# Gating two feed-forward blocks at once, with another order and other sums for the seven-product form

## The chip, the core and the metric

The kernel runs on one core of one Trainium2 chip. The core has a matrix engine (TensorE, PE in the profile, with its weight loads as PEld), a vector engine (VectorE, DVE), an activation engine (ScalarE, ACT), a general engine (GpSimd, POOL), a queue engine that issues transfers (SyncE, SP), and 16 DMA engines. Work is held in SBUF; matrix products go to PSUM, eight banks of 512 float32 columns in each of 128 partitions. The metric is the device time of one execution in microseconds (us), and less is better.

## What is computed

Two layers, each made of a feed-forward half, a mixer and a second feed-forward half, on 256 positions of 1024 channels in float32:

```python
D_MODEL, SEQ, DEPTH, D_FF = 1024, 256, 2, 2816

def rms_norm(x, g):
    return x * lax.rsqrt(jnp.mean(x * x, axis=-1, keepdims=True) + EPS) * g

def swiglu(h, w_gate_up, w_down):
    a, b = jnp.split(h @ w_gate_up, 2, axis=-1)
    return (jax.nn.silu(a) * b) @ w_down

def hybrid_layer(x, ...):
    x = x + 0.5 * swiglu(rms_norm(x, ffn1_norm), ffn1_w_gate_up, ffn1_w_down)
    h = rms_norm(x, mix_norm)
    z = h @ w_in                       # u, q, k, v and two gates
    y_pool = multiscale_pool(u, pool_w, pool_scale)
    y_attn = moba_attention(rope(rms_norm(q)), rope(rms_norm(k)), v)
    merged = gate0 * (y_pool @ w_branch_pool) + gate1 * (y_attn @ w_branch_attn)
    x = x + merged @ w_out
    return x + 0.5 * swiglu(rms_norm(x, ffn2_norm), ffn2_w_gate_up, ffn2_w_down)
```

The change lies in the feed-forward halves. There are four of them, called stages 1 to 4 here; mixers stand between stages 1 and 2 and between 3 and 4, so stage 3 follows stage 2 directly.

## The kernel before

**Precision.** Every float32 operand of a product is split into a high part (`hi`, the operand in a reduced float32 format) and the rest (`lo`). ACT writes the high part as a copy, DVE writes the rest as a subtraction (`split`, L173 and L174; `halves`, L245 and L246, for activations). A product is then a matmul of the high weights with high and low activations side by side (512 columns) and one of the low weights with the high activations (256 columns), in `chain`.

**The feed-forward half.** The 2816 inner channels are 22 blocks of 128. A block has one weight unit of 1 MB (gate and up columns). `unit` hands out the next split unit, `fetch` issues the next load on SP into one of four `raw` buffers and splits it in two halves; the split parts have room for three units, so a unit can be split once the unit three places earlier has been multiplied. `pair` multiplies a block (32 matmuls) into two PSUM banks, and `drain` brings it to SBUF: ACT copies the part from the low activations (L222), DVE adds the rest (L223), into a tile `ab` of gate (256 columns) and up (256 columns). `post` gates a block: DVE scales both halves by the norm factor `r` (L398), ACT takes Silu of the gate half (L400), DVE multiplies it with the up half (L401), and `halves` splits the product into one of the tiles `ga` (blocks 0 to 7), `gc` (8 to 11), `gd` (12 to 15) and `gb` (16 to 21). The factor `r` comes from the sum of squares `acc` by two matmuls against ones (`factor_spread`, also per token in `factor_tokens`). The down projection then runs over 8 output rows f, and for each over all 22 blocks; `add_x` (L566 on) adds half of each row to `x`, and `prep` (L284, L285, L293, L294) makes the next stage's input `hx` from it. That input is not yet scaled by the norm factor, which is why `r` comes after the product.

**The forms.** In stages 2 to 4 blocks 12 to 15 are not multiplied directly. They are a 2 by 2 product of blocks (two token halves, two halves of the 1024 input channels, two column pairs), done with seven products instead of eight, Strassen's method in Winograd's form. The seven are called "1" to "7" and cost 16 matmuls each. The weight sums that they need are made by the DMA: `sum_form` sends a quadrant of the weights from POOL's queue into a buffer, later quadrants with addition (`accum_op`), and after each sum has been split the next one is added on top. Buffer "a" lies where `gd` will be and serves forms 1, 5, 6 and 4 in this order; buffer "b" lies in `gb` and serves 3 and 7; form 2 is a plain load. The sums of x (`x_forms`, L443 on) are made after block 3: eight ACT copies (L447), four DVE sums (L451 to L454) and four splits (L458, L459). `strassen` multiplies a form (`by_tokens`) into a PSUM bank and combines the products on DVE in SBUF tiles `p1`, `p5` and `c35`; `gated` gates a quarter of the result (L485, L486), and `turned` transposes two quarters back on PE into `gd` (L493 to L496). `feed_order` holds the order of blocks and forms.

**The order of the work.** PE's order is the program's. The other engines' order is worked out ahead by a planner, which takes what it holds to be ready, by the place in the program; `behind` forbids it to place one operation ahead of another. On the chip each engine's queue then runs in that order, and an operation that waits holds all that stands behind it.

**Buffers.** `ab` tiles come from five buffers of 512 columns (tag "t512"), which the mixer's temporaries use as well; in stage 1 eight more lie in the tile of the mixer's gates. `uT`, the mixer's pooling input, has a place of its own.

Of the kernel before, what the change touches and what calls it, by code (L numbers as in the profile page):

```python
# [25 lines left out]
P = 128  # L26
# [20 lines left out]
GROUP = 12  # L47
XF = 3
SHIFT = 16
FIRST = 5  # L50
FORMS = {
    "1": ("a", False, "11"), "3": ("b", False, "22"), "2": ("c", False, "21"), "5": ("a", True, "12"),
    "7": ("b", True, "12"), "6": ("a", True, "22"), "4": ("a", True, "21"),
# [3 lines left out]
def feed_order():  # L57

    return [0, 1, 2, 3, 4, 5, "1", 6, "3", 7, "2", 8, "5", 9, "7", 10, 11, "6", 16, 17, 18, "4", 19, 20, 21]
# [10 lines left out]
def trunk_kernel(ctx: ExitStack, tc: tile.TileContext, x_in, w_in, pw_in, qkn_in, rope_in, mask_in, band_in, out):  # L70
# [35 lines left out]

    plan = []
    for base in (0, FU, LU, LU + FU):
# [30 lines left out]
    sums_at = {}  # L139

    def sum_form(base, f):

        n = base + GROUP
        q = {"11": (n, 0), "12": (n + 2, 0), "21": (n, 1), "22": (n + 2, 1)}
        at, add, src = FORMS[f]
        if at == "c":
            sums_at["c"] = raws.tile([P, 2 * HALF], F32, name="raw", tag="raw")
        z = sums_at[at].rearrange("p (i c) -> p i c", i=2)
        u, kh = q[src]
        w = w_in[u:u + 2, :, kh * HALF:(kh + 1) * HALF].rearrange("u p c -> p u c")  # L150
        if add:
            nc.gpsimd.dma_start(z, w, accum_op=OP.add)
        elif at == "c":
            nc.sync.dma_start(z, w)
        else:
            nc.gpsimd.dma_start(z, w)
        _, hi, lo = buffers(False)
        z = z.rearrange("p i (k c) -> p i k c", c=2 * P)
        for h in range(2):
            a = z[:, :, 2 * h:2 * h + 2, :]  # L160
            hv, lv = (t[h].rearrange("p (k i c) -> p i k c", i=2, c=2 * P) for t in (hi, lo))
            act(hv, a, AF.Copy)
            tt(lv, a, hv.bitcast(F32), op=OP.subtract)
        return hi, lo
# [102 lines left out]
    uT = const.tile([P, NW, PAD + S], F32, name="uT")  # L267
    nc.gpsimd.memset(uT[:, :, :PAD], 0.0)
# [95 lines left out]

    def bc2(a):
        return a.unsqueeze(1).to_broadcast([P, 2, a.shape[-1]])

    def ffn(after, n0=0, end=False, col=None):
# [6 lines left out]

        room("ga", 0, 8)
        room("gc", 8, 4)
        abs_, more = {}, []

        def wide(n):  # L380
            if n0 and len(abs_) in range(5, 13):
                if not more:
                    more.extend(eight(F32, "ab"))
                abs_[n] = more.pop(0).rearrange("p (a s) -> p a s", s=S)
            else:
                abs_[n] = tmp.tile([P, 2, S], F32, name="ab", tag="t512", bufs=5)
            return abs_[n]
# [8 lines left out]
        def post(n):  # L396
            ab = abs_[n]
            scaled = tt(ab, ab, bc2(r[0]), op=OP.mult)  # L398
            sg = small.tile([P, S], F32, name="sg", tag="sg", bufs=2)
            act(sg, ab[:, 0, :], AF.Silu)  # L400
            tt(sg, sg, ab[:, 1, :], op=OP.mult)  # L401
            halves(gs[n], sg)
            return scaled

        if n0:
            room("gd", 12, 4)
# [6 lines left out]
            for i in range(n0 + 1, NF + 1):  # L413
                if i < NF:
                    pair(unit(), wide(i))
                    fetch()
                todo = range(done, min(done + (2 if i % 3 == 2 else 1), i) if i < NF else NF)
                done = todo.stop
                for n in todo:
                    scaled = post(n)  # L420
                    if i == n0 + 1:
                        behind(scaled, drained[-1])
        else:
# [9 lines left out]
            sums_at["a"] = acts.tile([P, 2 * HALF], F32, name="sa", tag="gd")  # L433
            pre = acts.tile([P, 12 * S], F32, name="pre", tag="gb")
            sums_at["b"] = pre[:, :NK * S]
            vt = acts.tile([P, 2, GW], F32, name="vt", tag="v")
            tk = [acts.tile([P, 2, GW], F32, name="tk", tag="tok", bufs=2) for _ in range(2)]
            p1, p5, c35 = tk[0][:, 0], tk[0][:, 1], tk[1][:, 0]
            xg = [t.rearrange("p a (b s) -> p (a b) s", s=S) for t in tk]
            gq = {tn: vt[:, tn // 2, tn % 2 * S:(tn % 2 + 1) * S] for tn in range(4)}  # L440
            sf = {}

            def x_forms():  # L443

                late = drained[-1]
                for k in range(NK):
                    behind(act(xg[k // 4][:, k % 4, :], x[:, k, :], AF.Copy, scale=gain[:, l_of[0], col + k:col + k + 1]), late)  # L447
                (a11, a21), (a12, a22) = ([z[:, :, t * P:(t + 1) * P] for t in range(2)] for z in xg)
                s1, s2 = (pre[:, (8 + 2 * i) * S:(10 + 2 * i) * S].rearrange("p (k s) -> p k s", s=P) for i in range(2))
                s3, s4 = (vt[:, i, :].rearrange("p (k s) -> p k s", s=P) for i in range(2))  # L450
                tt(s1, a22, a21, op=OP.subtract)  # L451
                stt(s2, s1, -1.0, a11, op0=OP.mult, op1=OP.subtract)
                tt(s3, a11, a21, op=OP.subtract)
                stt(s4, s2, -1.0, a12, op0=OP.mult, op1=OP.subtract)  # L454
                fs = iter(eight(F32R, "sf", SHIFT))
                for n, z in (("5", s1), ("3", s4), ("6", s2), ("7", s3)):
                    sh, sl = (next(fs).rearrange("p (k s) -> p k s", s=P) for _ in range(2))
                    act(sh, z, AF.Copy)  # L458
                    tt(sl, z, sh.bitcast(F32), op=OP.subtract)  # L459
                    sf[n] = [(sh[:, k, :], sl[:, k, :]) for k in range(4)]  # L460
                for n, k0, t in (("1", 0, 0), ("2", 4, 0), ("4", 4, 1)):
                    sf[n] = [tuple(hx[:, k, j, t * P:(t + 1) * P] for j in range(2)) for k in range(k0, k0 + 4)]
# [17 lines left out]
            def gated(c, t, n, sign):  # L480
# [5 lines left out]
                stt(by_half(gq[2 * t + n]), c[:, :, 1, :], sc, by_half(sg), op0=OP.mult, op1=OP.mult)  # L486

            def turned(n):
# [5 lines left out]
                g = gt["gd"][:, 2 * n:2 + 2 * n]  # L494
# [5 lines left out]
            def strassen(f):  # L500

                b = {"1": "a", "2": "a", "5": "e", "3": "h", "6": "g", "7": "f", "4": "f"}[f]
                fresh = b not in bank
                if fresh:
                    bank[b] = quarter("p" + b).rearrange("p a s -> p (a s)")
                z = bank[b]
                by_tokens(f, z, fresh)
                if f == "1":
                    act(p1, z, AF.Copy)
                elif f == "2":  # L510
                    gated(z, 0, 0, 0)
                elif f == "5":
                    act(p5, z, AF.Copy)
                    tt(c35, bank["h"], p5, op=OP.add)
                elif f == "6":
                    tt(p1, z, p1, op=OP.add)
                    tt(c35, c35, p1, op=OP.add)
                    gated(c35, 0, 1, 1)
                    tt(p5, p5, p1, op=OP.add)
                    gated(p5, 1, 1, 1)  # L520
                elif f == "7":
                    tt(p5, z, p5, op=OP.add)
                    room("gb", 16, NF - 16)
                elif f == "4":
                    tt(p1, z, p1, op=OP.add)
                    gated(p1, 1, 0, 0)
                    room("gd", 12, 4)

            late = []
            wait = [0, 1]  # L530
            for i, n in enumerate(feed_order()[2:]):
                if isinstance(n, str):
                    strassen(n)
                    if n == "4":
                        late += [[1, 1], [2, 0]]
                    continue
                pair(unit(), wide(n))
                fetch()
                if n == XF:
                    x_forms()  # L540
                for m in wait[:2]:
                    post(m)
                wait = wait[2:] + [n]
                for z in late:
                    z[0] -= 1
                    if z[0] == 0:
                        turned(z[1])
            for m in wait:
                post(m)
        gs = [gs[n] for n in range(NF)]  # L550
        for b in range(NK * NF):
# [9 lines left out]
            if k == NF - 1:  # L561
                add_x(f, ps, f < NK - 1 or not end)
                after(f)

    def add_x(f, ps, two):
# [29 lines left out]
    def norm_rope(z, g):  # L595

        ms = small.tile([P, 2 * NH], F32, name="ms", tag="ms", bufs=2)
        for t in range(2):
            sq = tmp.tile([P, NH, DH], F32, name="sq", tag="t512", bufs=5)
# [9 lines left out]
        for t in range(2):  # L609
            zt = z[:, t, :].rearrange("p (h d) -> p h d", d=DH)  # L610
            tt(zt, zt, ri[:, t * NH:(t + 1) * NH].unsqueeze(2).to_broadcast([P, NH, DH]), op=OP.mult)
            sw = tmp.tile([P, NH, DH], F32, name="sw", tag="t512", bufs=5)
# [68 lines left out]
    def mix(l, after):  # L681
# [12 lines left out]
        nc.sync.dma_start(pw, pw_in[l])  # L694
        gates = [z.rearrange("p (a s) -> p a s", s=S) for z in eight(F32, "gates")]
# [151 lines left out]
        def mixed(f):  # L847
            mg = tmp.tile([P, 2, S], F32, name="mg", tag="t512", bufs=5)
# [78 lines left out]
    for l in range(L):  # L927
        l_of[0] = l
        ffn(lambda f: prep(f, l, C_GM), len(w3) if l == 0 else 0, col=C_G1)
# [4 lines left out]
        if l + 1 < L:  # L934
            ffn(lambda f: prep(f, l + 1, C_G1), col=C_G2)
        else:
            ffn(lambda f: nc.sync.dma_start(out[:, f, :], x[:, f, :]), end=True, col=C_G2)
# [90 lines left out]
```

## Time and profile before

| | us |
|---|---|
| three runs | 1000.77, 1002.33, 2642.07 |
| their median | 1002.33 |
| the profiled execution | 1001.17 |
| its span | 999.4 |
| PE busy in it | 994.3 |
| DVE busy | 811.2 |
| ACT busy | 646.3 |

The span runs from the first to the last instruction of the profiled execution; the time of that execution is 1.77 us longer. Busy times of PE are modelled at their ends, so the chain of work that ended last says more than the busy share: it follows the last instruction back, at each step to what released it or to the instruction before it on its engine. In the timelines a row is the start, the duration, the engine, the line, what it writes and reads, and in brackets how long its engine had been idle before and who ended that. The rows of groups give count, total busy time and the mean of one in ns. The granted clock of PE is 1.00 in every stretch looked at.

Which stretch of time is which stage can be read from the chain: PE's product for the norm factor (two matmuls named `ss`) stands at 31.2, 334.8, 510.0 and 828.7 us, near the start of stages 1 to 4.

### The profile page before, as it was taken

The numbers are of one execution on the slowest core, as the hardware profiler recorded it, in microseconds if no ns is written. First come the engines' busy times: TensorE is split into PE (matmuls) and PEld (weight loads), VectorE is DVE, ScalarE is ACT, GpSimd is POOL, SyncE is SP. The second block draws the span as 40 slices with busy tenths as digits, with TensorE's granted clock in tenths as the row PEclk, the third lists the DMA queues.
The fourth block names the chain that finished last, engine by engine and source line by source line (L and its number), as shares of the span: only waits on it lengthen the run. The fifth ranks groups of instructions, "written<-read, shape, count | busy, mean of one in ns | idle before, by whom it ended". The sixth has DMA issues, their size and how long they took to land.

```text
span 999.4 us, 16145 instructions
## 1 busy us (share of the span) xinstructions
PE 994.3 (99%) x6336; PEld 903.0 (90%) x6336; DVE 811.2 (81%) x1220; ACT 646.3 (65%) x1026; POOL 35.1 (4%) x64
## 2 busy tenths in 40 slices
PE   9999999999999999999999999999999999999998
PEld 8888888898899988899998889998988999888988
DVE  6998866598978899886689988666988888989752
ACT  7876655567756786665578666556677567767541
POOL 0000000002000000000000000000020000000000
PEclk9999999999999999999999999999999999999999
DMA  8865555643556578765577876555544575785640
GB/s 296 313 211 204 204 188 207 206 150 140 194 204 250 184 173 282 211 210 184 197 259 175 283 205 212 182 202 184 188 179 178 171 255 177 225 223 202 223 148 22
DMA packets 34156, 202.34 MB, mean 202 GB/s; under 512 B 3488, under 2 KB 4768, under 8 KB 13088
## 3 DMA queue, kind: packets, MB, share of 16 engines
q1 hardware_dynamic: 29184, 182.44, 51.3%
q0 software_dynamic: 4896, 18.88, 9.0%
q8 instruction: 49, 0.80, 0.3%
q14 instruction: 27, 0.22, 0.1%
HBM read 200.26 MB, written 1.05 MB: 201 GB/s over the span
## 4 chain that ended last, share of the span: by engine, by line
PE 99%; DMA 0%; ACT 0%; DVE 0%; SPq 0%; issue 0%
PE ps L100 78%; PE pt L100 7%; PE two L100 4%; PE pe L100 2%; PE pa L100 2%; PE pf L100 2%; PE sc L100 1%; PE pg L100 1%; PE ph L100 1%; PE pt L667 1%; PE y L100 1%; DMA raw<-w 0%; PE tp L623 0%; PE pt L493 0%; PE st L100 0%; PE ss L100 0%
## 5 line engine op out<-in xcount | busy, mean ns | idle before, releaser
L100 PE MATMUL ps<-hx,hi 128*128 128x512 f32 x1504 | 507.0, 384 | 0.8 <-ACT hi L173 0.8
L174 DVE TENSOR_TENSOR lo<-raw,hi 128x1024 fp32r<-128x1024 f32 (+2 forms) x343 | 409.0, 1199 | 118.6 <-ACT hi L173 116.5
L173 ACT ACTIVATE hi<-raw 128x1024 fp32r<-128x1024 f32 (+2 forms) x343 | 352.1, 1035 | 201.5 <-PE ps L100 141.5
L100 PE MATMUL ps<-hx,lo 128*128 128x256 f32 x1504 | 411.1, 273 | 0.0
L100 PEld LDWEIGHTS ps<-hx,hi 128*128 128x128 f32 x1504 | 282.3, 188 | 51.3 <-ACT hi L173 1.1
L100 PEld LDWEIGHTS ps<-hx,lo 128*128 128x128 f32 x1504 | 282.6, 188 | 0.3 <-DVE lo L174 0.3
L100 PE MATMUL ps<-ga,hi 128*128 128x512 f32 (+1 forms) x264 | 87.0, 376 | 0.0
L100 PE MATMUL ps<-ga,lo 128*128 128x256 f32 x256 | 69.9, 273 | 0.0
L100 PE MATMUL ps<-gb,hi 128*128 128x512 f32 (+1 forms) x198 | 65.6, 376 | 0.0
L100 PE MATMUL pt<-hi,hx 128*128 128x512 f32 x192 | 65.1, 385 | 0.0
L100 PEld LDWEIGHTS ps<-ga,hi 128*128 128x128 f32 x264 | 49.0, 188 | 8.3
L398 DVE TENSOR_TENSOR ab<-ab,r 128x512 f32<-128x512 f32 x76 | 52.0, 687 | 0.9
L100 PE MATMUL pt<-lo,hx 128*128 128x256 f32 x192 | 52.6, 274 | 0.0
L100 PE MATMUL ps<-gb,lo 128*128 128x256 f32 x192 | 52.4, 273 | 0.0
L223 DVE TENSOR_TENSOR ab<-ps,ab 128x512 f32<-128x512 f32 x74 | 50.7, 686 | 0.9
L400 ACT ACTIVATE sg<-ab 128x256 f32<-128x256 f32 x76 | 31.3, 415 | 27.5 <-DVE ab L398 24.2
L100 PEld LDWEIGHTS ps<-ga,lo 128*128 128x128 f32 x256 | 48.1, 188 | 0.0
L100 PE MATMUL ps<-gc,hi 128*128 128x512 f32 (+1 forms) x132 | 44.3, 376 | 0.0
L100 PE MATMUL ps<-gd,hi 128*128 128x512 f32 (+1 forms) x132 | 44.3, 376 | 0.0
L100 PE MATMUL ps<-mk,hi 128*128 128x256 f32 x256 | 44.1, 275 | 0.0
L222 ACT ACTIVATE ab<-ps 128x512 f32<-128x512 f32 x74 | 43.0, 581 | 0.5 <-PE ps L100 0.5
L100 PEld LDWEIGHTS ps<-gb,hi 128*128 128x128 f32 x198 | 36.7, 188 | 6.2
(226 smaller groups left out, 1444.4 us busy)
## 6 DMA issues: line engine op xcount, KB each, us to landing
raw<-w SPq DMA_DIRECT2D x167, 1024.0 KB, 4.9
sa<-w POOLq DMA_DIRECT2D x12, 1024.0 KB, 9.8
pre<-w POOLq DMA_DIRECT2D x6, 1024.0 KB, 10.7
raw<-w SPq DMA_DIRECT2D x16, 256.0 KB, 5.3
out_dram<-gx SPq DMA_DIRECT2D x8, 128.0 KB, 1.9
gx<-x SPq DMA_DIRECT2D x3, 256.0 KB, 5.9
qk<-pw SPq DMA_DIRECT2D x2, 256.0 KB, 2.7
gx<-x SPq DMA_DIRECT2D x1, 300.0 KB, 2.8
```

Of the source, the lines that this page charges most:

```text
L100: return keep(nc.tensor.matmul(*args, **kw))
L173: act(hi, w, AF.Copy)
L174: return tt(lo, w, hi.bitcast(F32), op=OP.subtract)
L222: act(t, ps[:, :, 1, :], AF.Copy)
L223: drained.append(tt(t, ps[:, :, 0, :], t, op=OP.add))
L398: scaled = tt(ab, ab, bc2(r[0]), op=OP.mult)
L400: act(sg, ab[:, 0, :], AF.Silu)
L667: keep(nc.tensor.transpose(pt[:, h, o * P:(o + 1) * P], pr[:, h, c * P:(c + 1) * P], ident))
```

## The change

- `post` gates two blocks at once. Their `ab` tiles are one tile of 1024 columns, from two buffers (tag "t1k") and a third that shares its place with `uT`; in stage 1 four such tiles lie in the gates' tile. The splits of the product are written for two blocks by one ACT and one DVE operation. Blocks are gated in pairs, so the even block of a pair waits for the odd one.
- In stages 1 to 3 (`late_r`) only the gate half is scaled by `r`. The up half stays unscaled through the down projection, and `add_x` multiplies each output row by `r`, with one DVE operation more. The gated quarters of the forms leave out the same factor. In stage 4 both halves are scaled as before, for two blocks at once.
- The forms come in the order 1, 2, 7, 6, 5, 3, 4, the first after block 2 and the last ahead of block 11. Forms 1, 6, 5 and 3 are summed in one PSUM bank and read out in between; 2, then 7 and 4, in another.
- The weight sums lie in two buffers, "a" in the place of `gc` (form 1, then 5) and "b" in the place of `gd` (forms 7, 6 and 4). Form 7's sum takes two transfers; forms 2 and 3 are plain loads on SP.
- The sums of x are still made after block 3, but form 7's first; the copies lie in `pre` and not in `tk`. The transposes of the forms' results come in the middle of block 11 and after it, and were after blocks 19 and 20.
- The mixer's temporaries are halves of "t1k" tiles, and `uT` is allocated and its padding cleared in each mixer.

```diff
-    return [0, 1, 2, 3, 4, 5, "1", 6, "3", 7, "2", 8, "5", 9, "7", 10, 11, "6", 16, 17, 18, "4", 19, 20, 21]
+    return [0, 1, 2, "1A", 3, "2A", 4, "7A", 5, 6, 7, "6A", 8, "5A", 9, "3A", 10, "4A", 11, 16, 17, 18, 19, 20, 21]
...
+NEAR = {
+    "1": (("11",), "a"), "5": (("12",), "a"), "7": (("12", "22"), "b"), "6": (("11",), "b"), "4": (("21",), "b"),
+    "2": (("21",), ""), "3": (("22",), ""),
+}
...
+    def near_sum(base, f):
+
+        qs, at = NEAR[f]
+        z = two_rows(near[at])
+        for i, q in enumerate(qs):
+            kw = {} if i == 0 and f in "17" else {"accum_op": OP.add}
+            nc.gpsimd.dma_start(z, quadrant(base, "A", q), **kw)
+
+    def sum_form(base, n):
+
+        f, g = n
+        if g == "A" and NEAR[f][1]:
+            z = near[NEAR[f][1]]
+            _, hi, lo = buffers(False)
         else:
-            nc.gpsimd.dma_start(z, w)
+            z, hi, lo = buffers()
+            nc.sync.dma_start(two_rows(z), quadrant(base, g, NEAR[f][0][0]))
...
             act(hv, a, AF.Copy)
             tt(lv, a, hv.bitcast(F32), op=OP.subtract)
+        if g == "A":
+            if f in "176":
+                near_sum(base, {"1": "5", "7": "6", "6": "4"}[f])
...
+    def wide_tile(k):
+
+        if k % 3 < 2:
+            z = tmp.tile([P, 4 * S], F32, name="ab", tag="t1k", bufs=2)
+        else:
+            z = acts.tile([P, 4 * S], F32, name="ab", tag="uT")
+        return z.rearrange("p (b a s) -> p b a s", b=2, s=S)
...
         def post(n):
-            ab = abs_[n]
-            scaled = tt(ab, ab, bc2(r[0]), op=OP.mult)
-            sg = small.tile([P, S], F32, name="sg", tag="sg", bufs=2)
-            act(sg, ab[:, 0, :], AF.Silu)
-            tt(sg, sg, ab[:, 1, :], op=OP.mult)
-            halves(gs[n], sg)
+
+            ab = abs_[n // 2]
+            g, u = ab[:, :, 0, :], ab[:, :, 1, :]
+            if late_r:
+                scaled = tt(g, g, bc2(r[0]), op=OP.mult)
+            else:
+                z = ab.rearrange("p b a s -> p (b a) s")
+                scaled = tt(z, z, r[0].unsqueeze(1).to_broadcast([P, 4, S]), op=OP.mult)
+            act(g, g, AF.Silu)
+            tt(g, g, u, op=OP.mult)
+            name, i = place(n)
+            z = gt[name][:, i:i + 2]
+            act(z[:, :, 0, :], g, AF.Copy)
+            tt(z[:, :, 1, :], g, z[:, :, 0, :].bitcast(F32), op=OP.subtract)
             return scaled
...
+                tt(s3, a11, a21, op=OP.subtract)
+                tt(s1, a22, a21, op=OP.subtract)
+                parts_of("7", s3)
+                stt(s2, s1, -1.0, a11, op0=OP.mult, op1=OP.subtract)
+                parts_of("5", s1)
+                stt(s4, s2, -1.0, a12, op0=OP.mult, op1=OP.subtract)
+                parts_of("6", s2)
+                parts_of("3", s4)
...
-                b = {"1": "a", "2": "a", "5": "e", "3": "h", "6": "g", "7": "f", "4": "f"}[f]
+                b = ("x" if f in "1653" else "y") + g
...
                 elif f == "2":
-                    gated(z, 0, 0, 0)
+                    tt(p1, z, p1, op=OP.add)
+                    gated(p1, 0, 0, 0)
+                elif f == "6":
+                    act(w, z, AF.Copy)
                 elif f == "5":
-                    act(p5, z, AF.Copy)
-                    tt(c35, bank["h"], p5, op=OP.add)
-                elif f == "6":
-                    tt(p1, z, p1, op=OP.add)
-                    tt(c35, c35, p1, op=OP.add)
-                    gated(c35, 0, 1, 1)
-                    tt(p5, p5, p1, op=OP.add)
-                    gated(p5, 1, 1, 1)
-                elif f == "7":
-                    tt(p5, z, p5, op=OP.add)
-                    room("gb", 16, NF - 16)
+                    act(p1, z, AF.Copy)
+                    tt(p1, bank["y" + g], p1, op=OP.add)
+                    gated(p1, 1, 1, 1)
+                elif f == "3":
+                    gated(z, 0, 1, 1)
                 elif f == "4":
-                    tt(p1, z, p1, op=OP.add)
-                    gated(p1, 1, 0, 0)
+                    tt(w, z, w, op=OP.add)
+                    gated(w, 1, 0, 0)
...
+                if n % 2 and n > 1:
+                    post(wait[0])
+                    wait = [n - 1, n]
+            post(wait[0])
...
             act(t, ps[:, 1, :], AF.Copy)
+            if r is not None:
+                tt(t, ps[:, 0, :], t, op=OP.add)
+                stt(t, t, 0.5, r, op0=OP.mult, op1=OP.mult)
+                tt(x[:, f, :], x[:, f, :], t, op=OP.add)
+                return
             stt(t, t, 0.5, x[:, f, :], op0=OP.mult, op1=OP.add)
```

More of the change, by code (lines that the diff above doesn't have):

```diff
@@ L104, in banks @@
         return pool.tile([P, 2, 2, S], F32, name=name, tag="mm" if pool is pmm else "at2")
+    STAGES = (FU, LU, LU + FU)
     plan = []
-    for base in (0, FU, LU, LU + FU):
+    for base in (0, *STAGES):
         plan.extend(feed_units(base) if base else range(NF))
@@ L363, in eight, with half_tile, ffn @@
         return [z[:, i * GW:(i + 1) * GW] for i in range(NK)]
+    def wide_tile(k):
[4 more added lines that the diff above has]
+        return z.rearrange("p (b a s) -> p b a s", b=2, s=S)
+    spare_half = []
+    def half_tile():
+        if not spare_half:
+            z = tmp.tile([P, 2, GW], F32, name="th", tag="t1k", bufs=2)
+            spare_half.extend([z[:, 0], z[:, 1]])
+        return spare_half.pop(0)
     def bc2(a):
         return a.unsqueeze(1).to_broadcast([P, 2, a.shape[-1]])
-    def ffn(after, n0=0, end=False, col=None):
+    def ffn(after, n0=0, end=False, col=None, base=0):
         gs, gt = {}, {}
@@ L374, in room, with place @@
             gs.update({n0 + i: g[:, i] for i in range(m)})
+        def place(n):
+            name, first = next(z for z in (("gb", 16), ("gd", 12), ("gc", 8), ("ga", 0)) if n >= z[1])
+            return name, n - first
         room("ga", 0, 8)
-        room("gc", 8, 4)
         abs_, more = {}, []
+        late_r = not end
         def wide(n):
[L381 to L387, printed above, removed]
+            m = n // 2
+            if m not in abs_:
+                k = len(abs_)
+                if n0 and 3 <= k < 7:
+                    if not more:
+                        z = acts.tile([P, NK * GW + 4 * SHIFT], F32, name="ab", tag="gates")
+                        more.extend(z[:, i * 4 * S:(i + 1) * 4 * S].rearrange("p (b a s) -> p b a s", b=2, s=S) for i in range(4))
+                    abs_[m] = more.pop(0)
+                else:
+                    abs_[m] = wide_tile(k if k < 3 or not n0 else k - 4)
+            return abs_[m][:, n % 2]
         r = []
@@ L416, in ffn @@
                     fetch()
[L417 to L422, printed above, removed]
+                if i == NF or i % 3 != 1:
+                    for n in range(done, NF if i == NF else min(done + 2, i - 1), 2):
+                        scaled = post(n)
+                        done = n + 2
+                        if i == n0 + 1:
+                            behind(scaled, drained[-1])
         else:
@@ L530, in ffn @@
+            due = None
             wait = [0, 1]
-            for i, n in enumerate(feed_order()[2:]):
+            for n in feed_order()[2:]:
                 if isinstance(n, str):
-                    strassen(n)
-                    if n == "4":
-                        late += [[1, 1], [2, 0]]
+                    strassen(*n)
+                    if n[0] == "4":
+                        due = n[1]
                     continue
-                pair(unit(), wide(n))
-                fetch()
+                if due:
+                    pair(unit(), wide(n), lambda: turned(1, due), NK // 2)
+                    fetch()
+                    turned(0, due)
+                    due = None
+                else:
+                    pair(unit(), wide(n))
+                    fetch()
@@ L561, in ffn, with add_x @@
             if k == NF - 1:
-                add_x(f, ps, f < NK - 1 or not end)
+                add_x(f, ps, f < NK - 1 or not end, r[0] if late_r else None)
                 after(f)
-    def add_x(f, ps, two):
+    def add_x(f, ps, two, r):
         t = x[:, f, :]
@@ L694, in mix @@
         nc.sync.dma_start(pw, pw_in[l])
+        uT = acts.tile([P, NW, PAD + S], F32, name="uT", tag="uT")
+        nc.gpsimd.memset(uT[:, :, :PAD], 0.0)
         gates = [z.rearrange("p (a s) -> p a s", s=S) for z in eight(F32, "gates")]
@@ L934, in trunk_kernel @@
         if l + 1 < L:
-            ffn(lambda f: prep(f, l + 1, C_G1), col=C_G2)
+            ffn(lambda f: prep(f, l + 1, C_G1), col=C_G2, base=FU)
         else:
-            ffn(lambda f: nc.sync.dma_start(out[:, f, :], x[:, f, :]), end=True, col=C_G2)
+            ffn(lambda f: nc.sync.dma_start(out[:, f, :], x[:, f, :]), end=True, col=C_G2, base=LU + FU)
 def _feat(a):
```

100 lines of the change are left out of this document (40 added, 60 removed).

## The prediction

> **What bounds the kernel now.** I read the busy shares first, then the chain of work that ended last, then that chain in order of time, then the groups of instructions with shapes kept apart, and last the timelines of VectorE (DVE), ScalarE (ACT) and GpSimd (POOL) around each place that the change touches.
>
> ```profile
> span 999.4 us, 16145 instructions
> PE 994.3 (99%) x6336; PEld 903.0 (90%) x6336; DVE 811.2 (81%) x1220; ACT 646.3 (65%) x1026; POOL 35.1 (4%) x64
> PE 99%; DMA 0%; ACT 0%; DVE 0%; SPq 0%; issue 0%
> 31.39 152.03 PE ps L100 x912
> 438.03 72.00 PE ps L100 x432
> 534.71 2.72 PE pa L100 x16
> 537.43 5.34 PE ps L100 x32
> 542.77 2.69 PE ph L100 x16
> 931.86 64.25 PE ps L100 x406
> ```
>
> PE is the chain, end to end: 16 matmuls (a form) take 2.69 to 2.72 us, 32 (a block) 5.34 us, and 432 in a row take 72.00 us, 0.1667 us each, as do the 912. No block waits for anything. What the change can give is therefore small (PE idles 999.4 - 994.3 = 5.1 us, mostly before the first matmul and after the last); what it can take is a cover that runs out. The other fact is how full DVE is where the forms begin:
>
> ```profile
> 502.00:513.30 11.30, 11.30 (x72) 10.23 (x71) 7.63 (x11) 7.91 (x12) 0.73 (x1) 1.00 0.98 343
> 518.60:534.70 16.10, 16.10 (x98) 14.49 (x98) 15.12 (x26) 14.96 (x29) 1.22 (x1) 1.00 0.65 167
> 534.70:559.00 24.30, 24.30 (x147) 21.75 (x146) 24.04 (x31) 17.83 (x28) 2.42 (x2) 1.00 0.78 237
> ```
>
> The columns are PE, PEld, DVE, ACT and POOL busy time, granted clock, DMA share, GB/s. In the third feed-forward stage DVE is busy 15.12 of 16.1 us and 24.04 of 24.3, and PE still doesn't wait, because splits run up to three units ahead.
>
> **The parts, with their cost.**
>
> PE's work: still 18 full blocks and seven forms of 16 matmuls in each of stages 2 to 4, eight transposes, the same down projection. Keeping sums in PSUM takes DVE additions away and no matmul. Cost on the path: 0.
>
> DVE and ACT work for a pair of blocks. The prices:
>
> ```profile
> L174 DVE TENSOR_TENSOR lo<-raw,hi 128x1024 fp32r<-128x1024 f32 x328 | 400.6, 1227 | 117.4 <-ACT hi L173 115.4
> L398 DVE TENSOR_TENSOR ab<-ab,r 128x512 f32<-128x512 f32 x76 | 52.0, 687 | 0.9
> L401 DVE TENSOR_TENSOR sg<-sg,ab 128x256 f32<-128x256 f32 x76 | 31.6, 419 | 0.0
> ```
>
> Before, two blocks cost 2 x (0.687 + 0.419 + 0.419) = 3.05 us of DVE after their drains; now three 512-wide operations, 3 x 0.687 = 2.06. That is 0.99 us less per pair, and in the last stage, which still scales both halves (1.227 for 1024 elements), 0.45 less. Over 11 + 9 + 9 pairs and 9 pairs: 33 us. The forms need three additions of 0.687 fewer per stage (six before: one each after forms 5, 7 and 4, three after 6; now one each after 2, 5 and 4). The down projection gets one 256-wide operation more for each of 8 rows in three stages, 24 x 0.42 = 10 us, where DVE has idle time. All of it lies beside PE, so it is worth 0 on the path. New buffers (three pair tiles instead of five single ones, halves of one tile in the mixer): a pair tile is wanted again at least two blocks, 10.7 us, after its gating is issued, so 0. The clearing of the padding that moves into the mixer is one POOL operation ahead of sums that wait for PE anyway, 0.
>
> Step one on the path: the form that now needs x sums early. Form 7 reads them 2.7 + 5.34 = 8.0 us after block 3; before, form 3 was the first, 18.7 us after it. From the third stage before:
>
> ```profile
> 526.20 0.69 DVE L223 TENSOR_TENSOR ab<-ps,ab 128x512 f32<-128x512 f32 x1
> 527.53 0.69 DVE L453 TENSOR_TENSOR vt<-tk 128x512 f32<-128x512 f32 x1
> 529.35 0.69 DVE L459 TENSOR_TENSOR sf<-vt,sf 128x512 fp32r<-128x512 f32 x1
> 532.97 0.69 DVE L459 TENSOR_TENSOR sf<-vt,sf 128x512 fp32r<-128x512 f32 x1
> 534.51 1.22 DVE L174 TENSOR_TENSOR lo<-raw,hi 128x1024 fp32r<-128x1024 f32 x1
> 536.92 1.22 DVE L174 TENSOR_TENSOR lo<-raw,hi 128x1024 fp32r<-128x1024 f32 x1
> ```
>
> Form 1 starts at 534.71, four blocks after block 2, which so starts at 513.35. Before, block 3 ends at 524.03, and its drain runs on DVE at 526.20, 2.2 us later. In the new order block 3 ends at 513.35 + 5.34 + 2.72 + 5.34 = 526.75, form 2 at 529.5, block 4 at 534.8, form 7 at 537.5, and block 5 starts there. With the same lag the drain is at 528.9, and the split of form 7's x sum, 529.35 + 0.69 - 526.20 = 3.84 us on, is done by 532.8: in time for 534.8 by 2 us. The rest of the x work queues ahead of block 5's weight split. Before, the first weight split after it began 534.51 - 526.20 = 8.3 us after the drain. Of what stood between, block 4's drain, two scalings and a gating product fall out (3 x 0.69 + 0.42 = 2.5 us), and form 2's addition and gating product come in (at most 2 x 0.69 = 1.4). So it begins 7.2 us after the drain, at 536.1, and is done at 537.3, against 537.5 wanted: in time by 0.2 us, and no more. Without that cover, if the gating of blocks 0 and 1 also lands in this stretch (3 x 0.687 = 2.1 us), block 5 starts 1.9 us late. That gating can run ten microseconds sooner, once the norm factor is there, so I take 0; range 0 to 3 x 1.9 = 5.7 us over stages 2 to 4.
>
> Step two: the last pair. Block 20's gating used to run while block 21 was multiplied; now both wait for 21, and the down projection wants both at its 41st matmul. In stage 2:
>
> ```profile
> 445.52 0.68 DVE L223 TENSOR_TENSOR ab<-ps,ab 128x512 f32<-128x512 f32 x1
> 446.24 0.69 DVE L398 TENSOR_TENSOR ab<-ab,r 128x512 f32<-128x512 f32 x1
> 447.05 1.23 DVE L174 TENSOR_TENSOR lo<-raw,hi 128x1024 fp32r<-128x1024 f32 x1
> 448.19 0.42 DVE L401 TENSOR_TENSOR sg<-sg,ab 128x256 f32<-128x256 f32 x1
> 449.10 0.42 DVE L246 TENSOR_TENSOR gb<-sg,gb 128x256 fp32r<-128x256 f32 x1 [0.48 <-ACT gb L245]
> 129.75 0.42 DVE L246 TENSOR_TENSOR gb<-sg,gb 128x256 fp32r<-128x256 f32 x1
> 942.93 0.42 DVE L246 TENSOR_TENSOR gb<-sg,gb 128x256 fp32r<-128x256 f32 x1 [0.48 <-ACT gb L245]
> L222 ACT ACTIVATE ab<-ps 128x512 f32<-128x512 f32 x74 | 43.0, 581 | 0.5 <-PE ps L100 0.5
> L245 ACT ACTIVATE ga<-sg 128x256 fp32r<-128x256 f32 x32 | 13.0, 412 | 4.2 <-DVE sg L401 3.7
> ```
>
> Block 21 ends at 438.03 + 32 x 0.1667 = 443.36. Its last part was ready at 449.52, wanted (42 matmuls on) at 450.36. Now the wish is at 443.36 + 40 x 0.1667 = 450.03, and the chain grows by 0.27 (product 512 wide), 0.17 (copy, 0.581 for 0.412) and 0.27 (difference) = 0.71; the longer Silu still hides behind the split at 447.05. Ready 450.23: 0.2 us late. Stage 3 has the same spacing, 0.2. Stage 1's down projection starts at 183.42 - 352 x 0.1667 = 124.74, so 130.17 + 0.71 is in time for 131.4: 0. Stage 4 starts it at 931.86 + 5.34 = 937.2 and adds 0.54 for scaling 1024 elements: 943.35 + 1.25 = 944.6 against 943.9: 0.7. Sum 1.1 us; bounds 0, and one more weight split (1.23) ahead of the chain in each stage: 0.7 + 1.4 + 1.4 + 1.9 = 5.4.
>
> Step three: form 1's load, used three blocks earlier. In stage 3 its buffer is still read by the down projection, and ACT is about to turn the last row of x into the next stage's input:
>
> ```profile
> 500.34 0.74 POOL L156 DMA_DIRECT2D sa<-w  x1 [100.84 <-PE ps L100]
> 504.67 1.06 ACT L173 ACTIVATE hi<-raw 128x1024 fp32r<-128x1024 f32 x1 [1.05 <-issue]
> 505.64 0.49 ACT L284 ACTIVATE hx<-gx 128x256 fp32r<-128x256 f32 x1
> 506.91 0.48 DVE L285 SCALAR_TENSOR_TENSOR hx<-gx,hx 128x256 fp32r<-128x256 f32 x1
> sa<-w POOLq DMA_DIRECT2D x1, 1024.0 KB, 7.5
> sa<-w POOLq DMA_DIRECT2D x1, 1024.0 KB, 13.0
> ```
>
> The new buffer comes free four k steps earlier, 1.3 us, so the load goes out at 499.0 and lands between 506.5 and 512.0 (the shortest and longest landing of such loads). Form 1 is now the fourth unit, the one whose split stood at 504.67, ahead of the x row. The down projection ends at 438.03 + (32 + 352) x 0.1667 = 502.03, and block 0 wants that row 36 matmuls on, at 508.03; it is ready at 507.39, and the added DVE operation (0.42) makes that 507.8: 0. If the planner leaves the split where it stood, ACT stands still until the load lands, with the x row, the norm's input and block 0's drain behind it. I take 0, since the split has until 518.6 to be done and may go anywhere before; bound: 512.0 + 1.06 + 0.49 + 0.48 - 508.03 = 6.0. In stages 2 and 4 the mixer frees the buffers long before.
>
> **Sum.** 999.4 + 0 + 1.1 + 0 = 1000.5 us of span. The profiled execution took 1001.17 us, 1.77 more than its span, and lies 1.2 below the median of the three runs shown, 1002.33. Forecast: 1000.5 + 1.8 = 1002.3 us.
>
> **Rivals.**
> *All hidden.* DVE's lighter load (33 us) lets the last pair's steps start earlier; they are late by under 1 us. Against it: the added lengths sit in series, not in the load. Time 1001.2.
>
> *The pair's gating lands in the x stretch.* For it: DVE is full there (15.12 of 16.1 us). Against it: the gating is ready long before. 1002.3 + 5.7 = 1008.0.
>
> *ACT held by form 1's load in stage 3.* For it: the DMA share is 0.98 in just that window. Against it: ACT's waits before list none for a form's load. With a landing near 9 us, 508.0 + 1.06 + 0.49 + 0.48 - 508.03 = 2.0 us; time 1004.3, at most 1008.3.
>
> *The accumulating loads become the bound (slower).* The second buffer takes a plain load, an addition (form 7), and after each split another (6, then 4), in series. From form 7's split (about 529) to form 4's (574, 3.3 us before its start at 577.5) there are 45 us for two landings and a split of 3.3: landings decide from 20.9 us. The longest seen is 13.0. To cost 20 us over three stages (6.7 each) they would have to be 24.2: time 1023 or more. [...]
>
> *PE is not at its floor (faster).* The matmuls overlap, so 99% busy is no proof; weight loads sum to 903.0 us. Were PE to run at that rate, 999.4 - (994.3 - 903.0) = 908 us of span, 910 in all. Against it: 0.1667 us per matmul in every stage, wherever DVE is full or idle, and no matmul is removed. [...]
>
> **How the numbers follow.** Forecast 0.42, all hidden 0.23, gating in the x stretch 0.17, ACT held 0.14, accumulating loads 0.03, PE faster 0.01. About 2% is what a measurement of this kernel tells from no change: 20 us. The first four lie within it: 0.96; slower 0.03; faster 0.01. The range starts at 1000.0 (all hidden, and the 1.2 us by which the profiled execution and the median differ) and ends at 1010.0: the gating's 1008.0 and ACT held at its bound, 1008.3, with half the bound of step two's rest (5.4 - 1.1 = 4.3) on top of either.
>
> **What would show it.** Right: PE's chain whole but for gaps under 1 us at the 41st matmul of the down projections of stages 2 to 4. Step one is wrong if block 5 or form 7 starts after a gap, step two if the last pair is ready before its matmul, step three if ACT waits for a DMA before the x row of stage 3. The forecast falls if a PE gap over 3 us stands anywhere, or if POOL's loads land later than 20 us.

## The result, and the profile after

The changed kernel takes 1014.63 us (median of four runs, 1012.46 to 1019.32) against 1002.22 before: the ratio is 1.0135, with an interval of 1.009 to 1.018. The ratio leaves out one slow execution of the kernel before, of 2642.07 us, so it isn't the quotient of these two medians. The change makes the kernel slower, by less than 2%, and its time lies 4.6 us above the upper end of the range. The profiled execution is the slowest of the four.

| us | before | after |
|---|---|---|
| profiled execution | 1001.17 | 1019.32 |
| its span | 999.4 | 1017.6 |
| PE busy | 994.3 | 1003.3 |
| DVE busy | 811.2 | 791.7 |
| ACT busy | 646.3 | 636.1 |

DVE is 19.5 us lighter and ACT 10.2 lighter, and the time is longer. PE has the same 6336 matmuls and is busy 9.0 us more. These are lines of the changed kernel's page: the span and the busy times; below them, two of PE's waits (in total, how often, the longest):

```profile
span 1017.6 us, 15991 instructions
PE 1003.3 (99%) x6336; PEld 907.1 (89%) x6336; DVE 791.7 (78%) x1121; ACT 636.1 (63%) x953; POOL 35.3 (3%) x65
...
PE ps L99 <- DVE gb L445: 6.5, 4, 1.6
PE ps L99 <- DVE hx L294: 2.4, 1, 2.4
```

Before, PE's chain was whole. Now it is broken in five places: four times by 1.6 us for the last pair's gated product (`gb`), once in each stage, and once by 2.4 us for the next stage's input (`hx`) at the start of stage 3. Together 8.9 us. Most of the rest of the 18.2 us between the two spans is PE working more slowly after these breaks.

**The stall in each stage's last pair.** The timelines of ACT, DVE and PE in stage 1 of the changed kernel:

```profile
129.44 0.63 ACT L440 ACTIVATE ab<-ab 128x512 f32<-128x512 f32 x1
131.10 1.06 ACT L184 ACTIVATE hi<-raw 128x1024 fp32r<-128x1024 f32 x1 [1.02 <-PE ps L99]
132.06 0.61 ACT L444 ACTIVATE gb<-ab 128x512 fp32r<-128x512 f32 x1
...
130.66 0.68 DVE L441 TENSOR_TENSOR ab<-ab 128x512 f32<-128x512 f32 x1
132.19 1.22 DVE L185 TENSOR_TENSOR lo<-raw,hi 128x1024 fp32r<-128x1024 f32 x1 [0.84 <-ACT hi L184]
133.33 0.68 DVE L445 TENSOR_TENSOR gb<-ab,gb 128x512 fp32r<-128x512 f32 x1
...
132.17 0.27 PE L99 MATMUL ps<-gb,lo 128*128 128x256 f32 x1
134.07 0.49 PE L99 MATMUL ps<-gb,hi 128*128 128x512 f32 x1 [1.62 <-DVE gb L445]
```

The pair's product (L441) is ready at 131.34. Its copy (L444) should follow on ACT at once, but ACT has begun a weight split (L184) at 131.10, after standing still for 1.02 us until PE freed that split's buffer. The copy starts at 132.06. Then the second part of the same weight split (L185, 1.22 us) stands ahead of the pair's last difference (L445) on DVE, which starts at 133.33. Without the split, copy and difference would have run from 131.34 to about 132.63. The split belongs to the down projection's fourth weight unit, which PE wants only at the 97th matmul, some 9 us after the 41st. The waits above give the same 1.6 us for the other three stages.

**The slower rhythm behind it.** The chain in order of time of the changed kernel, stages 1 and 3, and a window of 20 us in stage 1 of the changed kernel and then of the kernel before (columns as in the prediction's windows):

```profile
32.44 98.57 PE ps L99 x591
...
134.07 53.65 PE ps L99 x312
...
638.67 53.66 PE ps L99 x312
...
140.00:160.00 20.00, 20.00 (x119) 17.70 (x118) 13.26 (x19) 9.76 (x14) 0.00 (x0) 1.00 0.55 185
...
140.00:160.00 20.00, 20.00 (x122) 17.99 (x122) 13.40 (x20) 10.69 (x16) 0.00 (x0) 1.00 0.54 194
```

Up to the stall the 591 matmuls take 0.1668 us each. The 312 behind it take 0.1720, with nothing waited for and a granted clock of 1.00: 312 x 0.0053 = 1.65 us. So each stage's end costs 1.62 + 1.65, about 3.2 us.

**The stall at the start of stage 3.** POOL, the chain, ACT, DVE and PE of the changed kernel there, then windows behind it:

```profile
506.21 0.74 POOL L155 DMA_DIRECT2D sa<-w  x1 [128.17 <-PE ps L99]
506.21 8.82 DMA sa<-w
515.14 1.06 ACT L170 ACTIVATE hi<-sa 128x1024 fp32r<-128x1024 f32 x1 [4.50 <-DMA sa<-w]
516.10 0.49 ACT L293 ACTIVATE hx<-gx 128x256 fp32r<-128x256 f32 x1
517.37 0.48 DVE L294 SCALAR_TENSOR_TENSOR hx<-gx,hx 128x256 fp32r<-128x256 f32 x1
517.90 0.49 PE L99 MATMUL ps<-hx,hi 128*128 128x512 f32 x1 [2.42 <-DVE hx L294]
...
518.00:520.00 2.00, 2.00 (x9) 1.73 (x10) 0.69 (x3) 1.59 (x3) 0.58 (x1) 0.66 0.38 158
520.00:522.00 2.00, 2.00 (x10) 1.81 (x9) 1.74 (x2) 1.03 (x2) 1.19 (x2) 0.50 0.40 33
522.00:524.00 2.00, 2.00 (x14) 1.83 (x15) 1.23 (x1) 1.97 (x3) 0.68 (x1) 0.99 0.93 158
```

Form 1's load goes out only when the down projection has freed its buffer, at 506.21, and lands 8.82 us later. Its split stands on ACT ahead of the copy that the last row of x needs (L293), so ACT is idle for 4.50 us while the row waits behind the load. After the gap of 2.42 us the granted clock falls to 0.66 and 0.50 for about 2 us each: (0.34 + 0.50) x 2 = 1.7 us more, an estimate from these two figures that takes PE's pace to go with the clock. In the chain the 12 matmuls behind the gap take 3.57 us, 1.57 more than 12 x 0.1667 = 2.00, and the two of `ss` 0.43 where they took 0.23 before.

**The account.** From the places of the norm factor's product (`ss`) in the two chains, the changed kernel loses 3.0 us from stage 1's product to stage 2's, 7.4 from there to stage 3's (the end of stage 2 and the start of stage 3), 3.4 to stage 4's and 3.4 from there to the end. Another 1.05 us goes before the first product for the factor, where the first 16 matmuls took 4.90 us, not 3.24; in the seven experiments that start from the changed kernel and share that code, the long run of matmuls of stage 1 begins at 30.57 to 31.48 six times and at 32.57 once, here at 32.44 and before at 31.39. So it differs from one execution to the next and isn't put down to the change. Four stage ends of 3.2, 4.2 at stage 3's start and 1.05 are 18.1 of 18.2 us. The other three runs have spans of 1010.7 to 1013.0; they have no trace, so which of these terms was smaller in them isn't seen.

### The profile page after: what moved, and what is told of

Its sections match the earlier page's. It is cut to its first block, busy times and chain, and to the rows that moved or that the text cites. A ratio compares the mean times of both kernels' runs of the same rounds, so it can differ in the third digit from the quotient of the medians.

```text
span 1017.6 us, 15991 instructions
## 1 busy us (share of the span) xinstructions
PE 1003.3 (99%) x6336; PEld 907.1 (89%) x6336; DVE 791.7 (78%) x1121; ACT 636.1 (63%) x953; POOL 35.3 (3%) x65
## 3 DMA queue, kind: packets, MB, share of 16 engines
HBM read 203.40 MB, written 1.05 MB: 201 GB/s over the span
## 4 chain that ended last, share of the span: by engine, by line
PE 84%; issue 13%; DMA 1%; DVE 1%; ACT 0%; SPq 0%; ACTq 0%; POOLq 0%
PE ps L99 65%; PE pt L99 6%; PE two L99 4%; PE pxA L99 2%; PE pyA L99 2%; PE pe L99 1%; PE sc L99 1%; DMA sa<-w 1%; PE pt L727 1%; PE y L99 1%; DMA raw<-w 0%; DVE lo L185 0%; ACT hi L184 0%; PE tp L683 0%; PE st L99 0%
## 5 line engine op out<-in xcount | busy, mean ns | idle before, releaser
L185 DVE TENSOR_TENSOR lo<-raw,hi 128x1024 fp32r<-128x1024 f32 (+2 forms) x343 | 407.8, 1198 | 137.8 <-ACT hi L184 135.9
L99 PE MATMUL ps<-hx,hi 128*128 128x512 f32 x1504 | 509.9, 385 | 3.1 <-DVE hx L294 2.4
L184 ACT ACTIVATE hi<-raw 128x1024 fp32r<-128x1024 f32 (+2 forms) x343 | 352.6, 1036 | 243.9 <-PE ps L99 150.3
L99 PE MATMUL ps<-hx,lo 128*128 128x256 f32 x1504 | 412.5, 274 | 0.0
L99 PEld LDWEIGHTS ps<-hx,hi 128*128 128x128 f32 x1504 | 283.7, 189 | 54.4 <-DVE hx L294 2.7
L99 PEld LDWEIGHTS ps<-hx,lo 128*128 128x128 f32 x1504 | 284.0, 189 | 0.2 <-DVE lo L185 0.2
L99 PE MATMUL ps<-ga,hi 128*128 128x512 f32 (+1 forms) x264 | 88.8, 380 | 0.0
L99 PE MATMUL ps<-gb,hi 128*128 128x512 f32 (+1 forms) x198 | 67.6, 382 | 6.5 <-DVE gb L445 6.5
L99 PE MATMUL ps<-ga,lo 128*128 128x256 f32 x256 | 70.4, 275 | 0.0
L99 PE MATMUL pt<-hi,hx 128*128 128x512 f32 x192 | 64.5, 383 | 0.0
L99 PEld LDWEIGHTS ps<-ga,hi 128*128 128x128 f32 x264 | 48.9, 187 | 9.7
L99 PE MATMUL ps<-gb,lo 128*128 128x256 f32 x192 | 52.8, 275 | 0.0
L99 PE MATMUL pt<-lo,hx 128*128 128x256 f32 x192 | 52.4, 273 | 0.0
L99 PEld LDWEIGHTS ps<-gb,hi 128*128 128x128 f32 x198 | 36.7, 187 | 14.8 <-DVE gb L445 7.7
L99 PEld LDWEIGHTS ps<-ga,lo 128*128 128x128 f32 x256 | 48.0, 188 | 0.0
L99 PE MATMUL ps<-gc,hi 128*128 128x512 f32 (+1 forms) x132 | 45.1, 380 | 0.0
L99 PE MATMUL ps<-gd,hi 128*128 128x512 f32 (+1 forms) x132 | 45.1, 380 | 0.0
L99 PE MATMUL ps<-mk,hi 128*128 128x256 f32 x256 | 44.1, 275 | 0.0
L99 PEld LDWEIGHTS pt<-hi,hx 128*128 128x128 f32 x192 | 36.0, 188 | 6.4
L99 PEld LDWEIGHTS ps<-mk,hi 128*128 128x128 f32 x256 | 38.7, 188 | 0.0
## 6 DMA issues: line engine op xcount, KB each, us to landing
sb<-w POOLq DMA_DIRECT2D x12, 1024.0 KB, 10.2
```

The lines of the kernel that those rows point to most:

```text
L99: return keep(nc.tensor.matmul(*args, **kw))
L184: act(hi, w, AF.Copy)
L185: return tt(lo, w, hi.bitcast(F32), op=OP.subtract)
```

## The experiments

Main theory (A): what the change loses lies in the two stalls, a split ahead of the last pair's steps and form 1's split ahead of the x row. The rivals were that the slower rhythm has a cause of its own (B), that the row's longer addition is late in stage 3 (C), that the pair's steps are simply too long, whatever stands ahead (D), and that in stage 3 it is ACT's order and not the wait for the load (E). The kernel before took 1000.36 us on the chip of the first four experiments and 1000.48 on that of the other four.

**Blocks 20 and 21 gated one at a time again.**

```diff
-            post(wait[0])
+            post_one(wait[0])
+            post_one(wait[1])
```

(and in stage 1 likewise; `post_one` is `post` for one block)

> Blocks 20 and 21 are gated one at a time in all four stages, everything else as changed. Theory A (the pair's gating waits for block 21 and is then held on ACT and DVE by the first weight splits of the down projection): the four PE gaps of 1.6 us at the 41st matmul go, and with them the slower matmuls behind them (312 at 0.172 us instead of 0.1667); some 4 x 3.2 = 13 us less in a profile like the one of the changed kernel, so 1002 to 1006 us, with stage 3's gap before block 0's last matmuls left. Rival B (the slow matmuls have another cause, the larger gb writes or the DMA): only the gaps go, 4 x 1.6 = 6.4 us less, 1008.

Measured: 1004.55 us, ratio 1.0042 (1.0027 to 1.0057). All four waits for `gb` are gone, and the down projections run undisturbed. PE's wait, the chain in stage 1 and a window of this kernel:

```profile
PE ps L99 <- DVE hx L294: 2.7, 1, 2.7
...
30.76 152.00 PE ps L99 x912
...
511.00:513.00 2.00, 2.00 (x7) 1.67 (x7) 1.11 (x2) 1.35 (x2) 1.22 (x1) 0.50 0.02 8
```

Stage 1 is again 912 matmuls in 152.0 us. With the stall the slower rhythm goes too. B, which expected 1008, falls: all four runs lie between 1003.51 and 1005.12. The 4.2 us that are left are the stage 3 stall of 2.7 us and, behind it, a time of low granted clock (0.50 in the window shown).

**Form 1's split held behind block 0's drain.**

```diff
+            if f == "1":
+                behind(z_hi, drained[-3])
```

> Only the split of form 1's weights is placed behind block 0's drain. Theory A (ACT stands 4.5 us for form 1's load in stage 3, with the last row of x behind it): the PE gap of 2.4 us near the start of stage 3 goes, and the low clock after it: 2.4 to 4.2 us less, so 1010 to 1012. Rival C (the gap comes from the longer addition of the down projection's rows, three DVE operations for two): the gap stays at 2 us or more and the time at 1014.

Measured: 1009.52 us, ratio 1.0094 (1.0077 to 1.0111), just under the 1010 to 1012 expected. The wait for `hx` is gone, with the row's longer addition still there, so C falls. PE's waits and the chain in stage 1:

```profile
PE ps L99 <- DVE gb L447: 6.5, 4, 1.6
...
30.62 98.59 PE ps L99 x591
132.27 52.27 PE ps L99 x312
```

The same stall of 1.6 us is followed here by 312 matmuls in 52.27 us, 0.1675 each, and so in all four stages: a stall doesn't always bring the slower rhythm. This kernel loses 9.2 us and the one before it 4.2; the changed kernel lost 12.4, about their sum of 13.4.

**The fourth down unit's split held behind the last pair's gating.**

```diff
+                if b == 48:
+                    fetch(pin=gated_last[-1])
```

> The pair stays a pair; the splits of the down projection's fourth weight unit are placed behind the last pair's gating. Theory A (it is the order): the last part is ready near the 41st matmul, gaps 0 to 0.3 us in stages 1 to 3 and under 0.8 in stage 4, and matmuls at 0.1667 us where there is no gap; 1002 to 1006 us. Rival D (it is the length of the pair's chain, six operations on 512 columns): gaps of 1 us or more stay in all four stages, 1010 or more.

Measured: 1007.29 us, ratio 1.0072 (1.0057 to 1.0087), above the 1002 to 1006 expected. The 1.6 us waits are gone, so D falls as to the size of the stalls, but the expectation had left out stage 3's start, which still waits:

```profile
PE ps L99 <- DVE hx L296: 2.6, 1, 2.6
...
PE ps L99 <- DVE gb L448: 0.3, 1, 0.3
...
512.00:514.00 2.00, 2.00 (x16) 1.85 (x15) 1.40 (x2) 1.99 (x3) 1.22 (x1) 1.00 0.00 0
```

The last line is a window behind that gap: 2.6 us of standing still, and the clock stays at 1.00, as it does in every window from 506 to 516 us. And the slower rhythm is back in stages 3 and 4, with hardly any gap: the last 544 matmuls of stage 3 take 93.85 us, where they took 90.67 with blocks 20 and 21 single, and the last 334 of stage 4 take 53.70, where they took 52.52 with form 1 held.

**Both holds together.**

> Both placements together: form 1's split behind block 0's drain, the fourth down unit's splits behind the last gating. Theory A: all that the change lost is back, 1000.5 to 1003 us, PE's chain whole but for what is left in stage 4. If something else in the change costs time (form order, x sums, late norm factor, buffers), the time stays above 1005 and PE shows where.

Measured: 1006.49 us, ratio 1.0062 (1.0047 to 1.0077), again above what was expected, and above the 1005 from which something else in the change would have to cost time. In the down projections PE waits only once, 0.3 us in stage 4. PE's wait, the chain, the row of DVE that the 41st matmul of stage 1 needs, PE's rows from the 39th on (the 41st is that of 130.44), PE's two rows at the same place of stage 3, and the window of 20 us in stage 1:

```profile
PE ps L99 <- DVE gb L450: 0.3, 1, 0.3
...
30.57 155.20 PE ps L99 x912
...
129.65 0.69 DVE L450 TENSOR_TENSOR gb<-ab,gb 128x512 fp32r<-128x512 f32 x1 [0.70 <-ACT gb L449]
...
130.10 0.38 PE L99 MATMUL ps<-gb,hi 128*128 128x512 f32 x1
130.32 0.27 PE L99 MATMUL ps<-gb,lo 128*128 128x256 f32 x1
130.44 0.45 PE L99 MATMUL ps<-gb,hi 128*128 128x512 f32 x1
130.73 0.28 PE L99 MATMUL ps<-gb,lo 128*128 128x256 f32 x1
130.85 0.40 PE L99 MATMUL ps<-gb,hi 128*128 128x512 f32 x1
...
629.06 0.45 PE L99 MATMUL ps<-gb,hi 128*128 128x512 f32 x1
629.35 0.27 PE L99 MATMUL ps<-gb,lo 128*128 128x256 f32 x1
...
140.00:160.00 20.00, 20.00 (x115) 17.31 (x114) 13.79 (x22) 10.09 (x15) 0.00 (x0) 1.00 0.53 186
```

The pair's part is ready at 130.34, just as PE comes to it. The 41st matmul's start is followed by the next after 0.29 us in place of 0.22 (130.44 to 130.73), and from there the stage runs at about 0.177 us per matmul: 155.2 us for the 912 in place of 152.0. With single gating the 912 take 152.00 us, and the rhythm stays. So the pair's length leaves no margin even with nothing ahead of it, and a break of 0.07 us can be followed by a loss of 3 us. It need not be: in stage 3 of this same kernel the step is 0.29 us too (629.06 to 629.35), and the stage goes on at 0.167 (544 matmuls in 90.73 us). So it does in stage 1 with only the fourth unit's split held: a step of 0.29 us (131.18 to 131.47), and 152.12 us for the 912.

**Single gating and form 1 held.** The edits of the first two experiments in one kernel.

> Blocks 20 and 21 gated one at a time, and form 1's split behind block 0's drain. Theory A (the two stalls, with the slower rhythm and the low clock behind them, are all that the change lost): PE waits nowhere, all four down projections at 0.1667 us per matmul, ratio to before 0.998 to 1.002. If more of the change costs time (form order, x sums, norm factor): ratio above 1.003.

Measured: 1000.75 us, ratio 1.0005 (0.9996 to 1.0013). No wait for `gb` or `hx` is left, and the chain again has `31.48 152.00 PE ps L99 x912` in stage 1. The last pair's late product and the wait for form 1's load, with the slower rhythm and the low clock behind them, are all that the change lost; the 6 us that were left with both holds came from the last pair. What is left of the change (the other pairs gated together, forms in PSUM, the factor moved) neither costs nor gives more than the interval allows, about 0.1%.

**The same with the norm factor on both halves again.**

```diff
-        late_r = not end
+        late_r = False
```

> As the run with single gating and form 1's split placed later, but with both halves scaled by the norm factor at the gating in all stages, as before the change, and the rows of the down projection without it. Theory A (the factor's move is hidden beside PE): the same time as with the move, ratio 0.998 to 1.002. If the move is worth something: above 1.003; if its added operation on the rows costs something: below the other by more than 0.2%.

Measured: 1001.0 us, ratio 1.0008 (0.9999 to 1.0017). With or without the factor at the down projection, the time is the same within these intervals.

**Single gating, and form 1 by a plain load on SP.**

```diff
-    "1": (("11",), "a"), "5": (("12",), "a"),
+    "1": (("11",), ""), "5": (("11", "12"), "a"),
```

> Blocks 20 and 21 gated one at a time; form 1's weights come by a plain load on SP into the ring of raw buffers, and form 5's sum by two transfers into the first buffer; ACT's order in stage 3 stays that of the changed kernel, the split of form 1 ahead of the last row of x. Theory A (the wait was for a load that could not go out before the down projection let its buffer go): the gap in stage 3 is gone with the order unchanged, ratio 0.998 to 1.002. Rival E (the place of that split in ACT's order is enough to make the row late): a gap of 0.5 to 1 us stays in stage 3.

Measured: 1007.19 us, ratio 1.0065 (1.0052 to 1.0078), where at most 1.002 was expected. Stage 3's first gap is gone with ACT's order unchanged: form 1's split runs at 504.00 without waiting for a DMA. So it was the wait for the load that held ACT, and E falls. But form 7's two transfers, which now run beside form 5's two, are late. The chain, ACT, the wait of PE and a window of this kernel:

```profile
499.67 12.80 DMA sb<-w
512.76 17.48 DMA sb<-w
...
530.35 2.01 ACT L170 ACTIVATE hi<-sb 128x1024 fp32r<-128x1024 f32 x2 [7.67 <-DMA sb<-w]
...
PE pyA L99 <- ACT sf L517: 3.4, 1, 3.4
...
537.00:541.00 4.00, 3.42 (x9) 2.62 (x10) 4.00 (x8) 4.00 (x8) 0.00 (x0) 0.50 0.97 194
```

The two transfers took 12.80 and 17.48 us, where form 7's took 11.5 and 8.8 in the changed kernel and the longest landing seen before the change was 13.0. ACT stood still for 7.67 us and PE for 3.4, with a clock of 0.50 behind it. That the two transfers for form 5 are what slowed them is likely; no run tests it alone.

**The kernel before, with a longer chain ahead of the last split of block 21.** Two extra DVE operations in stage 1, one in stage 2, none in stage 3, three in stage 4.

```diff
+                for _ in range(DELAY.pop(0)):
+                    nc.vector.tensor_scalar(sg, sg, 1.0, None, op0=OP.mult)
```

> The kernel before, with extra multiplications by 1 (0.42 us each on DVE) ahead of the last split of block 21: two in stage 1, one in stage 2, none in stage 3, three in stage 4. In stages 2 and 4 the planner's order then has a weight split that waits for PE ahead of block 21's last operation; in stage 1 it has not. Theory A: no gap in stages 1 and 3 and 0.1667 us per matmul; gaps of 1 to 1.6 us at the 43rd matmul of stages 2 and 4, and there a rhythm of 0.1667 or above for the rest of the projection; 1002.5 to 1007 us. Rival D (a longer chain costs its own length and no more): stage 2 shows no gap, since it had 0.8 us to spare, and stage 4 one of at most 0.5 us.

Measured: 1004.7 us, ratio 1.0042 (1.0029 to 1.0055). Two operations in stage 1 cost nothing. One in stage 2 (0.29 us, with 0.84 to spare by the prediction's rows) costs a stall of 1.0 us, where D expected none. Three in stage 4 (0.95 us, with about 0.85 to spare) cost a stall of 0.9 us, where D allowed 0.5 at most, and the matmuls behind it run in the slower rhythm (58 in the 9.93 us from 980.07 to 990.00, 0.171 each; the kernel before has 0.1667). So D falls. PE's waits and DVE in stage 2:

```profile
PE ps L101 <- DVE gb L247: 1.9, 2, 1.0
...
448.28 0.29 DVE L405 TENSOR_SCALAR sg<-sg 128x256 f32<-128x256 f32 x1
449.34 1.23 DVE L175 TENSOR_TENSOR lo<-raw,hi 128x1024 fp32r<-128x1024 f32 x1 [0.77 <-ACT hi L174]
450.49 0.42 DVE L247 TENSOR_TENSOR gb<-sg,gb 128x256 fp32r<-128x256 f32 x1
```

With 0.29 us more, the weight split has slipped ahead of the block's difference, as in the changed kernel, whereas before the difference came first. It is the order that costs, not the length: in stage 2 a single operation, well inside the time to spare, costs three times its own duration. (The two in stage 1 would have been free by their length too.)

## Why the prediction was wrong

- **The bound** was right: PE's chain is the kernel, and the time moves only where it breaks or slows.
- **Work beside PE at 0** was right: gating in pairs but for the last pair, the factor, the forms in PSUM, the buffers, POOL's clearing. With the stalls removed the kernel stands at 1.0005 of the one before. DVE's busy time fell by 19.5 us; the terms of the prediction (33 less, 10 more, and nine additions of 0.69) make 29, but no time hung on it.
- **Step one** (form 7's x sums, 0) was right in spite of its small margin of 0.2 us. The sum for form 7 is split by 545.6 in stage 3 of the changed kernel, and the form and block 5 follow without a gap; the chain has:

```profile
546.62 2.69 PE pyA L99 x16
549.30 16.02 PE ps L99 x96
```

- **Step two** (the last pair, 1.1 us with a bound of 5.4) is the step that failed. Its arithmetic for the chain alone was not far off: without the split the part would be ready at 132.63 in stage 1, where PE would have wanted it at 132.28, 0.11 us after the matmul of 132.17: 0.35 us late, where the forecast was 0. With the split held behind the pair, PE's waits are 0 in stages 1 to 3 and 0.3 us in stage 4, against 0, 0.2, 0.2 and 0.7 in the forecast. The bound named the right intruder, one more weight split, but counted only its 1.23 us on DVE. The split also waits on ACT for PE to free a buffer and then holds ACT for 1.06 us ahead of the copy, so it came into the chain on both engines: 1.62 us in every stage, in stage 1 too, where 0 was taken. The prediction took the order before as given when it lengthened the chain. The second half of the loss, up to 1.65 us for the slower rhythm behind each stall, was not in the prediction at all: it took 0.1667 us per matmul as PE's floor after any wait.
- **Step three** (form 1's load, 0) failed too: the likely value taken was the wrong one. The rival "ACT held" described just what happened and gave 2.0 us at a landing near 9; measured were 2.4 us at a landing of 8.8. It had 0.14. (The shortest landing of such a load before the change was 5.6 us, ahead of stage 2, and not 7.5; nothing here hangs on it.) The reason for taking 0, that the split may go anywhere before 518.6, forgot that nothing moves it there: before, the split that stood ahead of the row was of a plain load and waited for no DMA; now it is of one that comes late. The fall of the clock behind the gap, by the estimate above 1.7 us, was not foreseen.
- **The accumulating loads** did not become the bound in the changed kernel. The plain-load experiment shows that such transfers can stretch to 17.5 us, short of the 24.2 that the rival needed.
- **The sum**: forecast 1.1 + 0 against 4 x 3.2 + 4.2 in the profiled execution. The upper end of the range took one mechanism at its bound and half of another; both stalls came at once, and each brought a slowdown of PE with it.

## What to carry to other kernels

Where one engine's chain is unbroken, price a longer side chain by what stands in each queue between its last steps and its deadline, on every engine that the intruder touches, not by adding durations: 0.29 us more cost 1.0 us because another operation moved ahead. An operation that must wait (for a buffer that PE still reads, 1.02 us on ACT here, or for a load, 4.50 us) should not stand in an in-order queue ahead of the row that PE needs next; hold it behind, or keep the last blocks' steps short. Here holding was enough for the load, but not for the last pair: 1006.49 us with both holds, 1000.75 with the last two blocks gated one at a time. And a short break of the matmul stream can cost as much again behind it as the break itself: 1.65 us behind one of 1.62 in stage 1 of the changed kernel.

## What was unexpected of the hardware

**Rhythms at full clock.** After a disturbance the matmuls of a down projection ran at 0.167, 0.171 to 0.172 or 0.177 us each, all at a granted clock of 1.00 (in windows over the changed kernel's four down projections, and as the mean of the whole execution of each experiment with a slower rhythm), and kept their rhythm to the stage's end, some 310 matmuls; the next stage was back at 0.167 (223 in 37.24 us in stages 3 and 4 of the changed kernel). A stall of 1.6 us was followed by 0.172 in the changed kernel and by 0.167 with form 1 held; a break of 0.07 us was followed by 0.177 in stage 1 and by 0.167 in stage 3 of the kernel with both holds. What picks the rhythm stays open.

**The granted clock after short gaps.** It fell to 0.50 behind gaps of 2.4 us (the changed kernel) and 2.7 us (blocks 20 and 21 single), and not behind one of 2.6 us (the fourth unit's split held), where it stayed at 1.00. So the length of the gap alone doesn't decide it; what does, no run here shows. The slower rhythms at a clock of 1.00 are another thing.
